# The last quarter of two down projections, from eight block products to seven

## The chip, the cores and the metric

The kernel runs on one core of a Trainium2 chip. The engines are TensorE (PE in the profile; its weight loads are PEld), VectorE (DVE), ScalarE (ACT), GpSimd (POOL) and SyncE (SP, which only issues DMAs here). The metric is the device time of one execution in microseconds; before the change the median of three runs is 987.07 us (986.94 to 987.56).

## The reference

The program computes two layers of a decoder on 512 tokens of width 1024, in float32. Layer 0 mixes with latent attention, layer 1 with sliding-window attention. After each mixer stands a feed-forward part, the one that the change touches:

```python
for l in range(DEPTH):                       # DEPTH = 2
    y = mixer_l(x)                           # latent attention, then banded attention
    x = layernorm(alpha * x + y, ...)
    x = layernorm(alpha * x + mlp(x, w_up[l], w_down[l]), ...)

def mlp(x, w_up, w_down):                    # 1024 -> 4096 -> 1024
    h = relu(x @ w_up)
    return (h * h) @ w_down
```

## The kernel before, in words

**Precision by split parts.** Nearly all matmuls are in a reduced fp32 format. To keep precision, each operand is split into a high and a low part: ScalarE copies the source into the format (the high part, line 77), and VectorE or GpSimd subtracts it from the source (the low part, line 81). A product is then three matmuls: high by high, high by low, low by high (`three`, line 109; all matmuls are issued on line 105). The order of the PE instructions is that of the program text: `pe` (line 86) keeps it. The instructions of the other engines are laid in order by a scheduler unless they are pinned the same way; SyncE's loads go through `pe` too.

**The feed-forward part, in blocks.** The hidden width of 4096 is cut into four blocks `q` of 1024. For each, the up product (named U) and the down product (named D) multiply a 2 by 2 arrangement of quarters by another one: tokens in two halves of 256, the inner width in two halves of 512, the outer in two halves of 512. A scheme of Strassen's kind does this in seven quarter products instead of eight: U'1 to U'7 and D1 to D7, each on sums and differences of quarters. Sums of activation quarters (`Factors.sum`, line 697) are made on VectorE; sums of weight quarters are made by DMAs that add as they land (`accum_op=ALU.add`, line 204, issued by GpSimd), one quarter onto the last in the same buffer (`queue_seven`, line 168). A quarter product of D is 2 token tiles by 4 inner tiles by 3 matmuls of 128x512; one of U is 24 pairs of 256-wide matmuls, that is 48.

**The order.** `FIRST_STEPS`, `STEPS` and `LAST_STEPS` (lines 39 and 40) write out the order of the quarter products: D of one block is woven with U of the next (the prime marks the next block). Weights pass through a ring of four split tiles: `weights` (line 336) prepares up to four entries of one stream ahead of the one in use, and an entry is split as soon as an older one is used up.

**The last block.** Block 3's down product has no next block to be woven with, and was not cut in seven. `LAST_STEPS` ends with U'6, U'7, U'4 and D4; after D6 the running sum `u2` is spread over the token tiles (`take`, `add_plain`); then `TokMajor(...).finish` (lines 521 to 590, called on line 955) multiplies four token tiles by the whole 1024 x 1024 weight block: 4 tiles x 2 halves of 512 columns x 8 inner tiles x 3 matmuls. Eight weight chunks of 512 KB are loaded for it. The first 512 columns run with the inner tiles outside, the second with the token tiles outside, so that each token tile is finished in turn and its layer norm (`layer_norm`, line 484) runs under the next tile's products. In layer 0 the transposes of tokens 0 and 1 for the next layer (`turn_tokens`, line 500) stand between the tiles. In layer 1 the last tile's second half is cut in two pieces of 256 columns, and `last_norm` (line 469) ends the kernel: two plain fp32 matmuls (lines 472 and 477) centre half of the tile on PE while VectorE does the other half.

Token tiles live in `xs[0..3]` (1024 columns each: `lows` are the first 512, `highs` the last); `stats` collects what the layer norm needs. PSUM has eight banks: six under the tag `mm`, two under `tr`.

Of the kernel before, what the change touches and what calls it, by code (L numbers as in the profile page):

```python
# [8 lines left out]
F32 = mybir.dt.float32  # L9
# [30 lines left out]
FIRST_STEPS, LAST_STEPS = "U'1 U'2 U'5 U'3 U'6 U'7 U'4 D'1 D'2", "U'1 D5 U'2 D3 U'5 D6 D7 U'3 U'6 U'7 U'4 D4"  # L40
# [8 lines left out]
def build(tc, nc, io, out):  # L49
    with ExitStack() as top:  # L50
# [6 lines left out]
        dr = top.enter_context(tc.tile_pool(name="dr", bufs=1, space=DRAM))  # L57

# [27 lines left out]
        def pe(ins):  # L86
            tc.keep_in_program_order(ins)
# [15 lines left out]
        def group(dst, pairs, first=True, last=True, **kw):  # L103
            for i, (st, mv) in enumerate(pairs):
                pe(nc.tensor.matmul(  # L105
                    dst, st, mv, start=first and i == 0, stop=last and i == len(pairs) - 1, **kw
                ))
# [174 lines left out]
        holds = []  # L282

        def mlp_stream(l):
# [7 lines left out]
            def down(q):  # L292
                return lambda r, c, jp: io["down"][l, q * 8 + 4 * c + 2 * (1 - r) + jp].rearrange(
                    "p (a b) -> p a b", a=2
                )

            add = {("U", q): queue_seven("up", "U", up(q)) for q in range(NFF)}
            add |= {("D", q): queue_seven("down", "D", down(q)) for q in range(NFF - 1)}
# [6 lines left out]
            for c in range(8):  # L305
                queue("down", io["down"][l, (NFF - 1) * 8 + c])
# [153 lines left out]
        def last_tokens(gb):  # L460
# [5 lines left out]
            nc.gpsimd.tensor_mul(xg, xs[NT - 1][:, 0:512], gb[0][:, 0:512])  # L466
            return minus, diag, xg, bank()

        def last_norm(gb, minus, diag, xg, b):

            x = xs[NT - 1]
            pe(nc.tensor.matmul(b, ident, xg, start=True, stop=False))
# [4 lines left out]
            pe(nc.tensor.matmul(b, diag, gb[0][:, 0:512], start=False, stop=True))  # L477
            late = slice(512, D)
            nc.vector.scalar_tensor_tensor(x[:, late], x[:, late], mv[:, 0:1], gb[0][:, late], ALU.subtract, ALU.mult)
            for c, src in ((late, x[:, late]), (slice(0, 256), b[:, 0:256]), (slice(256, 512), b[:, 256:512])):  # L480
                pin(nc.vector.scalar_tensor_tensor(x[:, c], src, r, gb[1][:, c], ALU.mult, ALU.add))
                nc.sync.dma_start(out[(NT - 1) * P : NT * P, c], x[:, c])

        def layer_norm(t, gb, dst):
# [9 lines left out]
            pin(nc.vector.scalar_tensor_tensor(x, x, mv[:, 0:1], gb[0], ALU.subtract, ALU.mult))  # L494
            state["norm"] = nc.vector.scalar_tensor_tensor(x, x, r, gb[1], ALU.mult, ALU.add)
            pin(state["norm"])
            if dst is None:
                nc.sync.dma_start(out[t * P : (t + 1) * P, :], x)
# [22 lines left out]
        class TokMajor:  # L521
# [25 lines left out]
            def finish(self, gb=None, dst=None, early=None, gb_at=None):  # L547
# [9 lines left out]
                if gb is not None:  # L557
# [3 lines left out]
                    for t in range(NT):  # L561
                        end = dst is None and t == NT - 1
                        n = 2 if end else 1
                        if end:
                            parts = last_tokens(gb)
                        for i in range(n):
                            c = slice(i * 512 // n, (i + 1) * 512 // n)
                            b = bank(512 // n)
                            for kp in range(4):
                                self.group(b, t, kp, ws[kp], c)  # L570
                            pinned[0] = early
                            with tc.high_priority():
                                self.evac(t, slice(512 + c.start, 512 + c.stop), b)
                            pinned[0] = False
                        pinned[0] = early
                        with tc.high_priority():
                            if end:
                                last_norm(gb, *parts)
                            else:
                                layer_norm(t, gb, dst)  # L580
                        if early:
                            prepare(early[t])
                        pinned[0] = False
                        if dst is not None and t in (1, 2):
                            with tc.high_priority():
                                dst.turn(t - 1)
# [9 lines left out]
        def run_steps(units, ahead, scores, turn, mix, fill, per, lag, rest):  # L596
# [5 lines left out]
            for u in range(-ahead, n):  # L602
# [9 lines left out]
                turn(*units[u])  # L612
                if u >= lag and (u - lag) % per == per - 1:
# [162 lines left out]
        def mlp(src, gb, dst, mp):  # L776
# [17 lines left out]
            class Block:  # L794
# [18 lines left out]
                def up(self, n):  # L813
# [4 lines left out]
                    key = {3: 3}.get(n) or own_bank[n]  # L818
                    for j in range(4):

                        b = self.bank(("U", key), j // 2)
                        wh, wl = w[j // 2]
                        for k in range(4):
                            c = slice(j % 2 * 512 + k * P, j % 2 * 512 + (k + 1) * P)
                            group(
                                b[:, j % 2 * 256 : j % 2 * 256 + 256],
                                three(wh[:, c], wl[:, c], src.part(n, 0)[:, k, :], src.part(n, 1)[:, k, :]),
                                n not in (2, 4) and k == 0 and j % 2 == 0, k == 3, skip_group_check=True,
# [838 lines left out]
```

## Time and profile before

| | |
|---|---|
| median of 3 runs | 987.07 us (986.94 to 987.56) |
| the profiled execution | 986.77 us, of which its span is 985.0 us |
| granted PE clock over the span | 1.000 |
| busy: PE, PEld, DVE, ACT, POOL | 978.4, 880.5, 773.4, 544.7, 235.7 us |
| DMA | 149.54 MB, mean 152 GB/s |
| last block of layer 0 with U'6, U'7, U'4, D4 before it | from 436.8 us |
| the same of layer 1 | 911.4 to 978.1 us |

Times in the views are microseconds from the span's start. A matmul's busy time overlaps the next one's, so a row's duration is not what it costs in a row of matmuls; that is the distance between starts. In views by window each engine's busy time is followed by its number of instructions. In the waits, the engine named after the arrow ended the idle time.

### The profile page before, as it was taken

How to read it: one execution, taken by the hardware profiler on the slowest of the kernel's cores; microseconds unless marked ns; L12 is line 12 of the kernel's file. 1: busy time of each engine (PE TensorE's matmuls, PEld its weight loads, DVE VectorE, ACT ScalarE, POOL GpSimd, SP SyncE). 2: the span in 40 equal slices, each digit the busy share in tenths (PEclk: the TensorE clock that was granted, in tenths of full speed). 3: DMA queues.
4: the chain of work that ended last, by engine and by line, in shares of the span. 5: the costliest groups of instructions: out<-in, count | busy, mean ns of one | idle time of the engine just before them, and what ended most of it. 6: DMA issues, size and time to landing. Idle time of an engine off the chain costs nothing.

```text
span 985.0 us, 15665 instructions
## 1 busy us (share of the span) xinstructions
PE 978.4 (99%) x6028; PEld 880.5 (89%) x6028; DVE 773.4 (79%) x1282; ACT 544.7 (55%) x842; POOL 235.7 (24%) x204
## 2 busy tenths in 40 slices
PE   9999999999999999999999999999999999999998
PEld 9888888998999999998898988889998998999986
DVE  6589858999778769887587788898886985888756
ACT  5557644467537637646136787445763763764720
POOL 1231101121212211310002898422221122033000
PEclk9999999999999999999999999999999999999999
DMA  7421236398878968973232212528997796897332
GB/s 264 146 89 44 91 124 199 59 225 218 156 181 235 183 141 237 226 125 120 94 108 86 97 65 98 191 44 181 256 179 134 236 197 117 225 264 140 82 128 86
DMA packets 60678, 149.54 MB, mean 152 GB/s; under 512 B 5259, under 2 KB 10300, under 8 KB 60604
## 3 DMA queue, kind: packets, MB, share of 16 engines
q0 software_dynamic: 24320, 58.73, 33.7%
q1 hardware_dynamic: 36140, 89.56, 26.0%
q8 instruction: 47, 0.77, 0.3%
q10 hardware_dynamic: 144, 0.26, 0.1%
q14 instruction: 27, 0.22, 0.1%
HBM read 146.41 MB, written 4.22 MB: 153 GB/s over the span
## 4 chain that ended last, share of the span: by engine, by line
PE 97%; DVE 2%; POOL 1%; ACT 0%; issue 0%; DVEq 0%; POOLq 0%
PE mm L105 89%; PE tr L105 5%; PE tr L1243 1%; PE tr L742 1%; POOL wl L81 1%; PE tr L1467 0%; PE tr L507 0%; DVE o L1503 0%; DVE mm L1431 0%; DVE pt L81 0%; PE tr L1007 0%; ACT wh L77 0%; DVE mm L1427 0%; PE mm L1148 0%; ACT p L1442 0%
## 5 line engine op out<-in xcount | busy, mean ns | idle before, releaser
L105 PE MATMUL mm<-wh,fac 128*128 128x512 f32 (+1 forms) x944 | 292.7, 386 | 0.0
L77 ACT ACTIVATE wh<-wq 128x1024 fp32r<-128x1024 f32 x164 | 173.7, 1060 | 184.7 <-PE mm L105 137.8
L81 DVE TENSOR_TENSOR wl<-wq,wh 128x1024 fp32r<-128x1024 f32 x164 | 199.2, 1220 | 67.5 <-ACT wh L77 66.6
L105 PE MATMUL mm<-xth,wh 128*128 128x256 f32 (+1 forms) x928 | 243.4, 290 | 0.0
L105 PE MATMUL mm<-xth,wl 128*128 128x256 f32 (+1 forms) x800 | 233.3, 292 | 0.0
L105 PEld LDWEIGHTS mm<-wh,fac 128*128 128x128 f32 x944 | 176.2, 188 | 35.5 <-DVE fac L81 0.6
L105 PE MATMUL mm<-xtl,wh 128*128 128x256 f32 (+1 forms) x672 | 197.1, 293 | 0.0
L105 PE MATMUL mm<-wl,fac 128*128 128x512 f32 (+1 forms) x472 | 182.3, 386 | 0.0
L105 PEld LDWEIGHTS mm<-xth,wh 128*128 128x128 f32 x928 | 168.6, 192 | 3.1
L105 PEld LDWEIGHTS mm<-xth,wl 128*128 128x128 f32 x800 | 153.2, 192 | 2.7
L105 PEld LDWEIGHTS mm<-xtl,wh 128*128 128x128 f32 x672 | 128.7, 191 | 3.0
L77 ACT ACTIVATE wh<-raw 128x1024 fp32r<-128x1024 f32 (+3 forms) x86 | 84.9, 989 | 79.3 <-PE mm L105 57.9
L204 POOL DMA_DIRECT2D wq<-in_up x64 | 77.6, 1238 | 200.3 <-DVE wl L81 193.0
L105 PEld LDWEIGHTS mm<-wl,fac 128*128 128x128 f32 x472 | 88.8, 188 | 16.6
L81 DVE TENSOR_TENSOR wl<-raw,wh 128x1024 fp32r<-128x1024 f32 (+2 forms) x64 | 74.3, 1169 | 30.6 <-ACT wh L77 29.6
L204 POOL DMA_DIRECT2D wq<-in_down x48 | 42.0, 874 | 189.1 <-DVE wl L81 183.2
L81 POOL TENSOR_TENSOR wl<-raw,wh 128x1024 fp32r<-128x1024 f32 (+2 forms) x22 | 47.1, 2143 | 90.8 <-ACT wh L77 65.2
L105 PE MATMUL mm<-wh,oh 128*128 128x512 f32 x128 | 50.7, 396 | 0.0
L105 PE MATMUL mm<-wl,oh 128*128 128x512 f32 x128 | 50.0, 391 | 0.2 <-POOL wl L81 0.2
L105 PE MATMUL mm<-wh,ol 128*128 128x512 f32 x128 | 50.2, 392 | 0.0
L443 POOL TENSOR_TENSOR rs<-mv,half 128x1 f32<-128x1 f32 x16 | 8.8, 552 | 168.1 <-DVE mv L488 163.4
L641 DVE TENSOR_TENSOR x<-mm,x 128x512 f32<-128x512 f32 (+1 forms) x49 | 32.9, 674 | 15.6 <-PE mm L105 15.5
(247 smaller groups left out, 1783.2 us busy)
## 6 DMA issues: line engine op xcount, KB each, us to landing
wq<-in_up POOLq DMA_DIRECT2D x64, 512.0 KB, 7.2
wq<-in_down POOLq DMA_DIRECT2D x48, 512.0 KB, 6.9
wq<-in_up SPq DMA_DIRECT2D x32, 512.0 KB, 6.8
raw<-in_down SPq DMA_DIRECT2D x28, 512.0 KB, 6.1
wq<-in_down SPq DMA_DIRECT2D x24, 512.0 KB, 5.9
raw<-in_up SPq DMA_DIRECT2D x16, 512.0 KB, 4.2
raw<-in_w_o SPq DMA_DIRECT2D x8, 512.0 KB, 3.3
raw<-in_w_sq SPq DMA_DIRECT2D x8, 512.0 KB, 3.2
```

The costliest lines, as they stand in the source:

```text
L77: high = nc.scalar.activation(dst_h, src, AF.Copy)
L81: low = (engine or nc.vector).tensor_sub(dst_l, src, f32(dst_h))
L105: pe(nc.tensor.matmul(dst, st, mv, start=first and i == 0, stop=last and i == len(pairs) - 1, **kw))
L204: state["added", key, a, more, jp] = nc.gpsimd.dma_start(half(a, jp), chunk(*more, jp), accum_op=ALU.add)
L443: state["rs"] = nc.gpsimd.tensor_tensor(r, v, half, ALU.pow)
L641: nc.vector.tensor_add(xs[t][:, c], b, xs[t][:, c])
L742: pe(nc.tensor.transpose(pt[:, a, :], xs[t][:, k * P : (k + 1) * P], ident))
L1243: pe(nc.tensor.transpose(pt[:, kb * P : (kb + 1) * P], p[:, kb * P : (kb + 1) * P], ident))
```

## The change

Both last blocks are now done in seven quarter products too, by a class `LastBlock`, in an order that `run` writes out for all engines.

- `LAST_STEPS` ends with D4. U'6, U'7 and U'4 of the last block are issued from the written plan, in halves (`up_half`), with their results' handling (`up_out`, `up_end`) as entries of their own.
- `run` is a list of (time, function) pairs, sorted by the time, which is only a key. While it is issued, all instructions of VectorE, ScalarE and GpSimd keep program order on their engine (class `Ordered`, flag `in_order`), not only PE's and SyncE's.
- The quarter products are 1, 2, 5, 3, 6, 7, each in two halves of one token tile (`times`, 12 matmuls), and the last one, on the quarter `a22`, in plain fp32: 4 matmuls a token tile on unsplit data (`low_left`); in layer 1 its second token tile is cut into two pieces of 256 columns.
- Sums that were made by adding results to `xs` afterwards are partly made in PSUM: ScalarE first copies `u2` or parts of `xs` into a bank (`into_bank`, `fill_end`), the product adds to it, and ScalarE copies results out (`copy_out`).
- The weights of products 1, 5 and 6 are one buffer that grows by accumulating DMAs (`grow`); those of 7 and of the plain product are sums which are prepared in DRAM: two plain copies and six accumulating DMAs, and two copies from DRAM to DRAM, a layer (`sum_quarters`), issued at written steps of the attention in layer 0 and of the feed-forward part in layer 1. `fetch` loads them.
- Of the twelve low parts of the weights, three (both of product 6, one of product 7) are made by GpSimd, as are four subtractions of token tiles' halves, three of them in the written plan's middle.
- Layer norms of the token tiles are cut in entries (`moments`, `centre`, `finish`). `last_norm` centres the second half of the last tile on PE instead of the first, and ScalarE and GpSimd scale and shift 256 columns of it, which ScalarE's queue stores.

The diff, cut to its core:

```diff
-FIRST_STEPS, LAST_STEPS = "U'1 U'2 ... D'2", "U'1 D5 U'2 D3 U'5 D6 D7 U'3 U'6 U'7 U'4 D4"
+FIRST_STEPS, LAST_STEPS = "U'1 U'2 ... D'2", "U'1 D5 U'2 D3 U'5 D6 D7 U'3 D4"
...
-                nc.vector.scalar_tensor_tensor(x[:, late], x[:, late], mv[:, 0:1], gb[0][:, late], ALU.subtract, ALU.mult)
-            for c, src in ((late, x[:, late]), (slice(0, 256), b[:, 0:256]), (slice(256, 512), b[:, 256:512])):
-                pin(nc.vector.scalar_tensor_tensor(x[:, c], src, r, gb[1][:, c], ALU.mult, ALU.add))
+            nc.vector.scalar_tensor_tensor(x[:, lows], x[:, lows], mv[:, 0:1], gb[0][:, lows], ALU.subtract, ALU.mult)
+            nc.scalar.activation(x[:, early], b[0], AF.Copy, scale=r)
+            nc.gpsimd.tensor_add(x[:, early], x[:, early], gb[1][:, early])
+            for c, src in ((lows, x[:, lows]), (late, b[1])):
+                nc.vector.scalar_tensor_tensor(x[:, c], src, r, gb[1][:, c], ALU.mult, ALU.add)
...
+                def product(self, b, f, t, w, first, cols=slice(0, 512)):
+                    tk = slice(t * P, (t + 1) * P)
+                    for m in range(4):
+                        if f is None:
+                            c = slice(m % 2 * 512 + cols.start, m % 2 * 512 + cols.stop)
+                            group(b, [(self.g["a22"][:, m, tk], w[m // 2][:, c])], False, m == 3, ...)
+                            continue
...
+            def sum_quarters(i, l, jp):
+            chunk = down(l, NFF - 1)
+            if i == 0:
+                pe(nc.sync.dma_start(sum_of(l, 7, jp), chunk(1, 1, jp)))
+            elif i == 1:
+                nc.gpsimd.dma_start(sum_of(l, 7, jp), chunk(0, 1, jp), accum_op=ALU.add)
+            elif i == 2:
+                pe(nc.sync.dma_start(sum_of(l, 4, jp), sum_of(l, 7, jp)))
+            else:
+                nc.gpsimd.dma_start(sum_of(l, 4, jp), chunk((0, 1)[i - 3], 0, jp), accum_op=ALU.add)
...
+            extra = sums_at(1, ((2, 2), (8, 14), (20, 20), (26, 32), (37, 43))) if layer else {}
...
+            todo = sums_at(0, ((0, 0), (3, 7), (12, 12), (13, 17), (21, 25)))
...
+                    at(8.7, self.factor_high, 3)
+                    at(9.18, self.factor_high, 6)
+                    at(10.28, self.grow, 6, 1, 1)
+                    at(10.85, self.into_bank, 5, 1, xs[1][:, highs])
+                    at(10.9, self.times, 5, 0, 5)
+                    at(13.27, self.copy_out, 1, 0, u2[0])
+                    at(13.28, self.high, 6, 0)
+                    at(13.28, self.high, 6, 1)
+                    at(13.6, self.times, 5, 1, 5)
+                    at(14.45, self.copy_out, 1, 1, u2[1])
+                    at(15.73, lambda: add_plain(2, highs, self.bank(("D", 5), 0)))
+                    at(15.73, self.fetch, 7)
+                    at(15.73, self.tops, 1)
+                    at(16.14, lambda: add_plain(3, highs, self.bank(("D", 5), 1)))
+                    at(16.3, self.times, 3, 0, 5)
+                    at(16.32, self.tops, 0)
...
+                    at(18.06, self.low, 6, 1, pool)
+                    at(19.0, self.times, 3, 1, 5)
+                    at(21.47, self.low, 6, 0, pool)
+                    at(21.8, self.times, 6, 0, 1)
+                    at(23.8, self.low, 7, 1, pool)
+                    at(27.2, self.times, 7, 0, 1)
+                    at(32.2, self.low_left, 0)
+                    at(34.6, self.times, 7, 1, 1)
+                    at(41.22, self.finish, 2)
+                    if end:
+                        at(38.0, self.low_left, 1, 0, 2)
+                        at(39.0, self.low_left, 1, 1, 2)
+                        at(39.44, self.left_out, 1, 0, 2)
+                        at(41.14, self.left_out, 1, 1, 2)
+                        at(42.58, lambda: parts.extend(last_tokens(self.gb)))
+                        at(44.0, lambda: last_norm(self.gb, *parts))
...
-            b = blocks[NFF - 1]
-            b.factor(2)
-            b.factor(1)
-            b.factor(4)
-            b.factor(0, True)
...
-            TokMajor(Hidden(), add_last, "down").finish(gb, dst, dst and (0, 0, 0, 1), 1)
-
+            in_order[0] = True
+            last.run(gb)
+            in_order[0] = False
```

More of the change, by code (lines that the diff above doesn't have):

```diff
@@ L46, with build @@
 C_ALL = 1024
-def build(tc, nc, io, out):
+def build(tc, core, io, out):
     with ExitStack() as top:
@@ L86, in pe @@
         def pe(ins):
-            tc.keep_in_program_order(ins)
+            if not (in_order[0] and ins.ins.engine in (mybir.EngineType.DVE, mybir.EngineType.Activation, mybir.EngineType.Pool)):
+                tc.keep_in_program_order(ins)
         pinned = [False]
@@ L290, in up @@
                 ].rearrange("c p x -> p c x")
[L292 to L295, printed above, removed]
             add = {("U", q): queue_seven("up", "U", up(q)) for q in range(NFF)}
[L298 removed]
+            add |= {("D", q): queue_seven("down", "D", down(l, q)) for q in range(NFF - 1)}
             preloads.append(add["U", 0].preload)
@@ L304, in mlp_stream @@
                     add[which, q](n)
-            for c in range(8):
-                queue("down", io["down"][l, (NFF - 1) * 8 + c])
+            for n in (6, 7, 4):
+                add["U", NFF - 1](n)
+            ends.append(len(stream))
         mlp_stream(0)
@@ L561, in finish @@
                     for t in range(NT):
[L562 to L575, printed above, removed]
-                        with tc.high_priority():
[L577 to L582, printed above, removed]
+                        b = bank()
+                        for kp in range(4):
+                            self.group(b, t, kp, ws[kp])
+                        pinned[0] = True
+                        with tc.high_priority():
+                            self.evac(t, slice(512, D), b)
+                        with tc.high_priority():
+                            layer_norm(t, gb, dst)
+                        prepare(early[t])
                         pinned[0] = False
-                        if dst is not None and t in (1, 2):
+                        if t in (1, 2):
                             with tc.high_priority():
@@ L612, in run_steps @@
                 turn(*units[u])
+                with behind([state["ex"]] if u in todo else None):
+                    for f in todo.get(u, ()):
+                        f()
                 if u >= lag and (u - lag) % per == per - 1:
@@ L817, in up @@
                     w.append(weights("up"))
-                    key = {3: 3}.get(n) or own_bank[n]
                     for j in range(4):
[L821 to L828, printed above, removed]
-                            )
+                        self.up_part(n, j, w[j // 2])
                         if j % 2:
                             self.up_out(n, j // 2)
+                            if j == 3:
+                                self.up_end(n)
                         if (self.q, n) == (0, 1) and j in (0, 3):
@@ L913, in mlp @@
+            blocks = [(LastBlock if q == NFF - 1 else Block)(q) for q in range(NFF)]
+            last = blocks[NFF - 1]
             steps = list(steps_of())
```

390 lines of the change are left out of this document (315 added, 75 removed).

## The prediction

> **What bounds the kernel now.** I read the engine shares and the chain first, then the two last blocks.
>
> ```profile
> span 985.0 us, 15665 instructions
> PE 978.4 (99%) x6028; PEld 880.5 (89%) x6028; DVE 773.4 (79%) x1282; ACT 544.7 (55%) x842; POOL 235.7 (24%) x204
> ...
> PE 97%; DVE 2%; POOL 1%; ACT 0%; issue 0%; DVEq 0%; POOLq 0%
> ```
>
> ```profile
> 436.00:503.00 67.00, 67.00 (x375) 58.52 (x374) 45.39 (x61) 26.37 (x28) 1.96 (x4) 1.00 0.31 94
> 911.00:978.00 67.00, 67.00 (x389) 59.24 (x388) 44.71 (x58) 22.33 (x22) 2.94 (x4) 1.00 0.30 95
> ```
>
> ```profile
> 911.38 5.76 PE tr L105 x48
> 917.13 61.01 PE mm L105 x336
> ...
> 978.17 0.43 DVE x L641
> ...
> 978.62 0.44 DVE bn L631
> ...
> 980.26 1.22 DVE x L481 x2
> ```
>
> TensorE (PE) is on 97% of the chain. The two windows cover the last block of each layer (columns: width, busy time of PE, weight load, VectorE, ScalarE, GpSimd, granted clock, DMA share, GB/s): PE never stops there, at full clock, while VectorE has 22 us free of 67. In the third view PE runs without a gap from U'6 (911.38) to 978.14. So time goes only as PE work goes, unless the new order makes PE wait; and after the last product there is a tail on VectorE.
>
> **The change, part by part.** *The matmuls.* Matmuls overlap, so the price is the distance of starts, not the duration.
>
> ```profile
> 959.75 0.62 PE L105 MATMUL mm<-wh,fac 128*128 128x512 f32 x2
> ...
> 960.43 0.62 PE L105 MATMUL mm<-wh,fac 128*128 128x512 f32 x2
> ...
> 977.37 0.28 PE L105 MATMUL mm<-wl,fac 128*128 128x256 f32 x1
> ...
> 977.73 0.28 PE L105 MATMUL mm<-wl,fac 128*128 128x256 f32 x1
> ...
> 977.96 1.02 PE L472 MATMUL mm<-xg,ident 128*128 128x512 f32 x2
> ```
>
> ```profile
> L472 PE MATMUL mm<-xg,ident x2: 592/592/593, 978.0 to 978.4; 128*128 128x512 f32 x2
> ```
>
> Three 512-wide matmuls of split parts take 960.43 - 959.75 = 0.68 us, 0.227 each; three 256-wide ones 0.36, 0.12 each. The one plain fp32 matmul in the kernel is two records that last 0.592 each and 1.02 together, so the second starts 0.43 after the first: 0.86 for a plain 512-wide matmul in a row of them, against 0.68 for the three that it replaces. Before, a layer's last block is 192 matmuls, 43.5 us (43.7 in layer 1, where the last 24 matmuls of 512 are halves: 24 x 0.12 in place of 12 x 0.227). After, it is six quarter products of 24, 144 x 0.227 = 32.7, and one of 8 plain matmuls, 8 x 0.86 = 6.9: 39.6. PE loses **3.9 us in layer 0 and 4.1 in layer 1**. Were a plain matmul only as dear as one split triple (0.68), it would be 5.3 and 5.5; at the bare duration of both records (1.18) it would be 1.4 and 1.6. I take 0.86, the start distance of this very form. Transposes and U'6, U'7, U'4 stay as many; D4 only moves ahead of U'6.
>
> *VectorE, ScalarE, GpSimd.*
>
> ```profile
> 929.83 1.22 DVE L81 TENSOR_TENSOR wl<-raw,wh 128x1024 fp32r<-128x1024 f32 x1
> 930.96 1.22 DVE L81 TENSOR_TENSOR fac<-a,fac 128x1024 fp32r<-128x1024 f32 x1
> ...
> 932.10 0.69 DVE L641 TENSOR_TENSOR x<-mm,x 128x512 f32<-128x512 f32 x1
> ```
>
> ```profile
> L81 POOL TENSOR_TENSOR wl<-raw,wh 128x1024 fp32r<-128x1024 f32 x14 | 34.7, 2477 | 58.6 <-ACT wh L77 35.6 <-PE mm L105 20.0 <-PE tr L1007 3.0
> ...
> L466 POOL TENSOR_TENSOR xg<-x,gb 128x512 f32<-128x512 f32 x1 | 1.3, 1282 | 46.0 <-DVE x L641 46.0
> ```
>
> ```profile
> 881.55 0.58 ACT L848 ACTIVATE a<-mm 128x512 f32<-128x512 f32 x1
> 883.46 1.06 ACT L77 ACTIVATE wh<-wq 128x1024 fp32r<-128x1024 f32 x1 [1.34 <-issue]
> ```
>
> A 1024-wide subtraction holds VectorE 1.13 us (start to start), a 512-wide one 0.6; ScalarE 1.06 and 0.58; GpSimd 2.48 and 1.28. Per block VectorE loses 8 low parts of weights and gets 9; 4 low parts of factors become 6; 4 sums of quarters are new, as are about two 512-wide adds: (1 + 2 + 4) x 1.13 + 1.2 = 9.1 us more. 45.4 + 9.1 of a window that shrinks to 63 is 87% busy: it fits, but each engine must now keep one written order. I walked that order with these durations, T = 0 at the first quarter product's first matmul. PE reaches product 2 at 5.4, 5 at 10.9, 3 at 16.3, 6 at 21.8, 7 at 27.2; the plain product's first half at 29.9. The tightest places: `factor_high(6)` on ScalarE waits for the third factor buffer until product 2 ends (10.9), then `into_bank(5,1)`, `copy_out(1,0)`, two highs of 6 and `copy_out(1,1)` end at 15.7; behind it on VectorE `tops(1)` runs to 17.1 and `add_plain(3)` to 17.7, and product 3's second half, which overwrites that bank, starts at 19.0. Its first half needs `add_plain(2)`, ready at 15.1, at 16.3. So the least cover is 1.2 us, and what is late beyond it PE waits for, one for one, as do all products behind. GpSimd's low parts of 6 run 15.2 to 20.1 against 21.8, that of 7 is done at 26 against 28.6. I count the waits at nothing by these covers, and put **0.5 us a layer** for what the walk can't see; the bounds are 0 and the 4.0 of the second rival.
>
> *DMA.* Per layer six accumulating transfers and four plain copies of 512 KB now build two sums in DRAM, in layer 0 during attention, in layer 1 during the MLP.
>
> ```profile
> q0 software_dynamic: 24320, 58.73, 33.7%
> q1 hardware_dynamic: 36140, 89.56, 26.0%
> ...
> wq<-in_up POOLq DMA_DIRECT2D x64, 512.0 KB, 7.2
> wq<-in_down POOLq DMA_DIRECT2D x48, 512.0 KB, 6.9
> ```
>
> ```profile
> 0.00:122.00 122.00, 121.01 (x676) 107.21 (x677) 95.31 (x276) 73.81 (x168) 24.68 (x26) 1.00 0.38 127
> ...
> 625.00:917.00 292.00, 291.81 (x1891) 267.20 (x1890) 240.64 (x265) 165.68 (x179) 68.83 (x63) 1.00 0.80 181
> ```
>
> All software transfers are the 112 accumulating ones: 0.337 x 985 / 112 = 3.0 us of all 16 engines each; a plain 512 KB is 0.26 x 985 x 0.524 / 89.56 = 1.5. So a layer gets 6 x 3.0 + 4 x 1.5 = 24 us. Layer 0's attention has 62% of 122 us free, layer 1's MLP 20% of 292, 58 us. No row shows an accumulation into DRAM; the upper bound I take is double, 48. Both fit on the whole, so 0. The cover of one late transfer is long: the weight split of 883.46 above had waited 1.34 us for its data, and, by the ring of four, it is U'5's second half, which PE reaches at 911.38 - 5.76 (U'3) - 2 x 24 x 0.227 (D7, D6) - 2.88 = 891.9, 6.0 us after its low part is out (883.46 + 1.06 + 1.3). GpSimd's issues and SyncE's loads are queued ahead by buffers, not by PE.
>
> *The tail.* The last block of layer 1 ends with left halves of 256 columns. `finish(2)` now stands on VectorE between the last token tile's statistics and their aggregation; before, it lay under PE work:
>
> ```profile
> 975.68 1.27 DVE L495 SCALAR_TENSOR_TENSOR x<-x,rs,gb 128x1024 f32<-128x1024 f32 x1
> ...
> 981.00 0.88 DVE L481 SCALAR_TENSOR_TENSOR x<-mm,rs,gb 128x256 f32<-128x256 f32 x2
> 981.04 1.30 SPq L482 DMA_DIRECT2D out<-x  x3
> ```
>
> That adds 1.27. One of two 256-wide steps (0.44) leaves VectorE for ScalarE and GpSimd; their path (diagonal product, 0.4 on ScalarE, about 0.65 on GpSimd, half of L466's 1.28) ends some 0.3 behind VectorE's. Sum **+0.9**, bounds 0.8 and 1.3.
>
> **Sum.** -3.9 - 4.1 + 1.0 + 0.9 = -6.1. The profiled execution took 986.77 us for its span of 985.0; 986.77 - 6.1 = 980.7. It lies 0.3 under the median of the runs (987.07), so **981.0**.
>
> **The rivals.** *GpSimd's subtractions hold VectorE up* (chance 0.15).
>
> ```profile
> 628.89 2.38 POOL L81 TENSOR_TENSOR wl<-raw,wh 128x1024 fp32r<-128x1024 f32 x1
> ...
> 629.15 3.21 DVE L81 TENSOR_TENSOR w_fac<-wq,w_fac 128x1024 fp32r<-128x1024 f32 x1
> ```
>
> Here a VectorE subtraction beside a GpSimd one took 3.21 us for 1.22: 2.0 lost. Three low parts a layer, each meeting one such subtraction, cost VectorE 6.0; the covers behind them (1.2 at product 3, 1.7 at 6, 2.6 at 7) leave perhaps 2 on PE: 981.0 + 2 x (2 - 0.5) = **984**. For it: the row. Against it: most VectorE work between T = 15 and 20 reads a bank, and such steps beside GpSimd keep their length. The Trainium skill (GPSIMD Engine Reference, Key points) says that GpSimd shares its SBUF interfaces with VectorE and collides with VectorE instructions that read two SBUF inputs; the trace agrees with its 3.21 us, and by that rule moving low parts to GpSimd frees VectorE of nothing while both read SBUF, and the time would be this rival's.
>
> *The written order makes ScalarE wait for a transfer* (0.10). `grow(6)` adds into a buffer that the highs of 6 read. If it went out where it stands, T = 10.3 and 11.2, and landed as late as this one:
>
> ```profile
> 909.70 1.20 POOL L204 DMA_DIRECT2D wq<-in_up  x1 [0.53 <-DVE wl L81]
> ...
> 917.92 1.06 ACT L77 ACTIVATE wh<-wq 128x1024 fp32r<-128x1024 f32 x1 [2.69 <-DMA wq<-in_up]
> ```
>
> 8.2 us later, the second high would end at 20.4, `copy_out(1,1)` at 21.0, `tops(1)` at 22.4, `add_plain(3)` at 23.0 against 19.0: 4.0 us a layer, 981.0 + 2 x 3.5 = **988**, no gain. Against it: only two subtractions stand ahead of it on GpSimd, and its buffer is free at 5.4.
>
> *The DMA engines fill up in layer 1* (0.15, slower). The mechanism is a backlog in the stretches with nothing free:
>
> ```profile
> 700.00:740.00 40.00, 40.00 (x246) 36.03 (x245) 34.36 (x34) 26.27 (x28) 10.07 (x10) 1.00 0.93 202
> ...
> 860.00:900.00 40.00, 40.00 (x245) 36.04 (x244) 33.07 (x34) 23.42 (x25) 10.08 (x10) 1.00 0.98 232
> ```
>
> The sums' steps 8, 26 and 37 fall into three such stretches, one a block. It decides from a delay of 6.0 us on, the cover above. At double price, with the copies of the neighbouring steps, a backlog of 10 leaves 4.0 on PE three times, 12.0: **993**. For it: shares of 0.93 and 0.98. Against it: the steps are six apart (over 30 us), and the stretches between have a quarter free.
>
> **How the numbers follow.** My forecast has 0.60; its own range is 979.0 (no waits, and plain matmuls a little cheaper) to 984. The first rival is still faster, the second within or just over the line, the third slower. A measurement here tells 0.2%, 2.0 us, from no change: faster is under 985.1, slower over 989.0. Faster 0.60 + 0.15 and a little of the second, 0.76; same 0.09; slower 0.15. The range leaves out the third rival and little else: from 977.2, no waits and plain matmuls at 0.68 (981.0 - 1.0 - 2.8), to 988.5, past the second rival; plain matmuls at 1.18 (986) lie inside.
>
> **What would show it.** Each last block has 144 matmuls of split parts, and 8 plain ones in 16 records (12 in 24 in layer 1, where four are halved), and the chain is still over 96% PE. A wait of PE on `x`, `u` or a bank from VectorE near product 3 means that the 1.2 us cover was short; subtractions of 2 to 3.2 us on VectorE beside GpSimd show the first rival; ScalarE waiting on a `wq` transfer ahead of the highs of 6 the second; PE waits on weights between 700 and 900 the third. The tail should run some 7.7 us from the last down matmul to the end, 6.8 before. I am wrong if a plain matmul's starts lie well off 0.43 apart.

## The result: 981.4 us, and the profile after

The changed kernel takes 981.41 us (median of four runs, 981.1 to 981.87) against 987.27 us for the kernel before beside it (986.94 to 987.56): a ratio of 0.9941, 95% interval 0.9924 to 0.9958. The forecast was 981.0. Run a second time on another occasion (called c_again below) it took 981.66 us (981.45 to 982.27), ratio 0.9942. The profiled execution took 981.28 us, 5.49 less than the one before. The total is right, but three of its terms are not: TensorE gained a little more than forecast, the waits that were allowed for did not come, and the tail lost 2.7 us instead of 0.9.

The page of the changed kernel, engine shares and shares of the chain:

```profile
span 979.4 us, 15632 instructions
PE 970.2 (99%) x5952; PEld 870.2 (89%) x5952; DVE 785.9 (80%) x1287; ACT 570.1 (58%) x884; POOL 278.9 (28%) x239
...
PE 94%; DVE 3%; DMA 1%; issue 1%; POOL 1%; ACT 0%; SPq 0%; POOLq 0%; DVEq 0%
```

The two last blocks as windows (width, then busy time of PE, weight load, VectorE, ScalarE, GpSimd, then granted clock, DMA share, GB/s), and two shorter ones from the end of layer 1's block:

```profile
436.00:501.00 65.00, 65.00 (x358) 54.68 (x356) 58.70 (x71) 41.90 (x51) 20.89 (x16) 1.00 0.61 177
907.00:970.00 63.00, 63.00 (x343) 54.04 (x343) 54.71 (x68) 36.34 (x44) 22.26 (x18) 1.00 0.59 161
...
937.00:952.00 15.00, 15.00 (x68) 12.43 (x67) 14.74 (x17) 9.41 (x13) 4.82 (x3) 1.00 0.48 123
...
962.00:969.70 7.70, 7.70 (x32) 5.85 (x32) 7.39 (x12) 0.60 (x1) 2.94 (x3) 1.00 0.25 100
```

PE is busy all through, as before. VectorE is busy 58.7 of 65 us in layer 0 and 54.7 of 63 in layer 1, where the prediction had worked out 54.5 of 63, and its free time is not spread: in layer 1 there are 0.3 us in the 15 us around product 3, and 0.3 us in the last 7.7. The chain of waits says the same (start, length, engine):

```profile
913.06 5.75 PE tr L126 x48
918.82 36.04 PE mm L126 x204
954.95 0.70 DVE x L69
...
966.23 1.92 DVE x L69 x2
968.23 1.27 POOL xg L69
969.50 2.73 issue
...
974.05 0.76 POOLq L1971
```

Before, the chain stayed on PE to the last product at 978. Now it leaves PE at 954.95, runs over VectorE, and ends on GpSimd's own closing instruction.

Matmuls matched one to one between the two traces show where the time went. The offset of the start of the same matmul, after minus before, is +0.66 us at the end of layer 0's attention; it falls from +0.66 to -3.68 across layer 0's last block (-4.34); it is -3.78 where layer 1's last block begins; it ends at -8.22 on the first matmul of `last_norm`, the first of the ident matmuls below (977.96 before, 969.74 after; -4.44 across the block). From that matmul to the end of the span the tail is 6.99 us before and 9.69 after: +2.70.

The tail of the changed kernel, by time (start, length, engine, operation; idle time before it and what ended that):

```profile
969.74 1.03 PE L496 MATMUL mm<-xg,ident 128*128 128x256 f32 x4
...
970.40 0.43 DVE L69 BATCH_NORM_STATS2 bn<-x 128x6 f32<-128x256 f32 x1
970.74 1.27 DVE L69 SCALAR_TENSOR_TENSOR x<-x,rs,gb 128x1024 f32<-128x1024 f32 x1
971.93 0.26 DVE L69 BATCH_NORM_AGGREGATE mv<-bn 128x2 f32<-128x24 f32 x1
...
974.08 0.72 POOL L69 TENSOR_TENSOR x<-x,gb 128x256 f32<-128x256 f32 x1 [1.25 <-ACT x L69]
974.84 0.35 ACTq L69 DMA_DIRECT2D out<-x  x1
```

And the closing instructions of GpSimd and SyncE, of the kernel after, and those of GpSimd in the kernel before (duration in ns, smallest, median and largest, first and last start):

```profile
L1971 POOLq DRAIN  x3: 40/93/4611, 974.0 to 979.2; - x3
L1971 SPq DRAIN  x3: 7/7/130, 977.2 to 978.9; - x3
```

```profile
L1663 POOLq DRAIN  x3: 40/102/3256, 979.4 to 984.7; - x3
```

The +2.70 has three pieces. Up to the aggregation it is +1.07: that is `finish(2)` (970.74). From the aggregation to the issue of the last store it is +0.1, where the prediction had taken 0.4 off. And +1.5 comes after the last store is issued: GpSimd's first closing drain begins at 974.05, lasts 4.61 us and ends at 978.66, while the last store has landed at 976.80. Before, the drain ended at 982.65, under the stores, the last of which landed at 984.00. Counted from the end of GpSimd's last instruction (979.98 before, 974.80 after) the drain takes 2.67 us before and 3.86 after; no term of the prediction held it. Not all of the 1.5 is the drain's: SyncE is through its own waits and its drain at 977.70, so GpSimd's drain holds the end up by 0.96 us. The other 0.6 lies in SyncE's closing waits, which run on for 0.9 us after the last landing, where they took 0.2 before.

### The profile page after: what moved, and what is told of

The parts are those of the page before. It is cut to its first block, busy times and chain, and to the rows that moved or that the text cites. A ratio compares the mean times of both kernels' runs of the same rounds, so it can differ in the third digit from the quotient of the medians.

```text
span 979.4 us, 15632 instructions
## 1 busy us (share of the span) xinstructions
PE 970.2 (99%) x5952; PEld 870.2 (89%) x5952; DVE 785.9 (80%) x1287; ACT 570.1 (58%) x884; POOL 278.9 (28%) x239
## 4 chain that ended last, share of the span: by engine, by line
PE 94%; DVE 3%; DMA 1%; issue 1%; POOL 1%; ACT 0%; SPq 0%; POOLq 0%; DVEq 0%
PE mm L126 86%; PE tr L126 5%; DMA sums<-in_down 1%; PE tr L1550 1%; DVE x L69 1%; PE tr L765 1%; PE tr L1775 0%; PE tr L539 0%; DVE o L1811 0%; DVE mm L1739 0%; POOL wl L101 0%; DVE bn L69 0%; DVE pt L101 0%; PE tr L1314 0%; DVE mm L1735 0%
## 5 line engine op out<-in xcount | busy, mean ns | idle before, releaser
L97 ACT ACTIVATE wh<-wq 128x1024 fp32r<-128x1024 f32 x158 | 167.3, 1060 | 183.3 <-PE mm L126 139.9
L101 DVE TENSOR_TENSOR wl<-wq,wh 128x1024 fp32r<-128x1024 f32 x158 | 192.1, 1221 | 79.2 <-ACT wh L97 78.7
L126 PE MATMUL mm<-wh,fac 128*128 128x512 f32 x736 | 232.2, 390 | 0.0
L126 PEld LDWEIGHTS mm<-wh,fac 128*128 128x128 f32 x736 | 138.3, 188 | 28.1
L126 PE MATMUL mm<-wl,fac 128*128 128x512 f32 x368 | 143.5, 390 | 0.0
L97 ACT ACTIVATE wh<-raw 128x1024 fp32r<-128x1024 f32 (+3 forms) x68 | 65.7, 970 | 38.0 <-PE mm L126 28.6
L126 PEld LDWEIGHTS mm<-wl,fac 128*128 128x128 f32 x368 | 69.2, 188 | 13.3
L101 DVE TENSOR_TENSOR wl<-raw,wh 128x1024 fp32r<-128x1024 f32 (+3 forms) x46 | 52.4, 1149 | 8.3 <-ACT wh L97 8.0
L126 PE MATMUL mm<-wx,fac 128*128 128x512 f32 x192 | 45.1, 392 | 0.0
L126 PEld LDWEIGHTS mm<-wx,fac 128*128 128x128 f32 x192 | 35.8, 188 | 7.7 <-DVE x L69 0.2
```

The costliest lines, as they stand in the source:

```text
L97: high = nc.scalar.activation(dst_h, src, AF.Copy)
L101: low = (engine or nc.vector).tensor_sub(dst_l, src, f32(dst_h))
L126: state["mm"] = nc.tensor.matmul(dst, st, mv, start=first and i == 0, stop=last and i == len(pairs) - 1, **kw)
```

## The experiments

Theory after the result: PE sets the time up to the last products, at the price of start distances; the covers on VectorE are as thin as walked; the tail is VectorE's work plus GpSimd's drain. Rivals: the drain is a sign only; the covers are wider; VectorE's room (55 of 63 us) would have carried more; the sums in DRAM cost something after all. Times are set against 981.41 and 981.66 of the changed kernel. Kernels that differ only in their end were up to 1.6 us apart ahead of it, so shifts of that size are read from the traces, by matched matmuls, and not from the medians alone.

**finish(2) ahead of the last half product.**

```diff
-                    at(41.22, self.finish, 2)
+                    at(39.0 if end else 41.22, self.finish, 2)
```

> finish(2) of layer 1 moved from behind the last token tile's statistics to before the last half product, under TensorE's work. Theory (the tail grew by two terms: finish(2) on VectorE's path, +1.1, and GpSimd's closing drain, +1.5, which hangs on GpSimd's last instruction): the tail falls from 9.7 to 8.6 us and the time by 1.1, to 980.3; the drain still ends last. Rival (GpSimd's drain alone sets the end, from something other than its last instruction, the stores in flight for instance): the tail stays at 9.7 and the time at 981.4. Second rival: VectorE has no 1.3 us to spare before the last half product, TensorE waits, and the time is 981.4 or more.

983.0 us (982.26 to 983.91), ratio 0.9957 [0.9943, 0.9970]. The tail is 10.16 us, 0.47 longer.

```profile
969.45 0.75 DVE L69 BATCH_NORM_STATS2 bn<-x 128x6 f32<-128x256 f32 x2
969.49 1.27 POOL L69 TENSOR_TENSOR xg<-x,gb 128x512 f32<-128x512 f32 x1 [0.28 <-DVE x L69]
970.12 1.73 DVE L69 SCALAR_TENSOR_TENSOR x<-x,rs,gb 128x1024 f32<-128x1024 f32 x1
971.02 1.03 PE L496 MATMUL mm<-xg,ident 128*128 128x256 f32 x4
971.77 0.41 DVE L69 TENSOR_TENSOR x<-mm,u 128x256 f32<-128x256 f32 x1
```

The theory falls and the second rival holds in part: PE did not wait, but there was no idle time on VectorE to put `finish(2)` into. Everything behind it, the additions of the last half product's results among it, came later, and beside a GpSimd multiplication it took 1.73 us for 1.27: the aggregation begins 2.64 us after the first ident matmul, 2.19 in the changed kernel. In this stretch VectorE, not PE, sets the time.

**The end without ScalarE's and GpSimd's share.**

```diff
-            nc.scalar.activation(x[:, early], b[0], AF.Copy, scale=r)
-            nc.gpsimd.tensor_add(x[:, early], x[:, early], gb[1][:, early])
-            for c, src in ((lows, x[:, lows]), (late, b[1])):
+            for c, src in ((lows, x[:, lows]), (early, b[0]), (late, b[1])):
...
-            nc.scalar.dma_start(out[(NT - 1) * P : NT * P, early], x[:, early])
```

> In last_norm the 256 columns of the end that went over ScalarE and GpSimd go over VectorE as the other 256 do, and SyncE issues all of the stores; nothing of the tail is left on GpSimd. Theory: GpSimd's closing drain then runs long before the end and the last store ends the kernel, as before the change; one more 256-wide step of 0.44 us on VectorE is paid back: the tail falls from 9.7 to some 8.2 us, the time by 1.1 to 1.6, to about 980.0. Rival (the drain is a sign and not the cause, and the stores themselves end later after the change): the tail stays at 9.7 or grows by 0.4, time 981.4 to 981.9.

981.86 us (980.64 to 982.24), ratio 0.9942 [0.9930, 0.9955]; the tail is 8.74 us, 0.95 shorter.

```profile
L1968 POOLq DRAIN  x3: 40/93/4454, 973.8 to 979.8; - x3
```

GpSimd's last instruction now ends at 974.43 and its drain, 3.86 us later again, at 978.29; the last store, issued at 976.34, lands at 978.40 and SyncE's closing waits end at 978.8. The last store lands 7.06 us after the first ident matmul in both kernels. So the drain is hidden, the tail shrinks although VectorE does 0.4 us more, and the drain was a cause and no sign. It gives 0.95 where 1.1 to 1.6 was expected, since SyncE's closing waits come right behind: from the issue of the last store to the end it is still 0.7 us longer than in the kernel before. The median shows none of it: the profiled run lost 1.6 us ahead of the tail, most of it in one place that is read below, under the run without sums.

**Both edits.**

> The edits of the two kernels above together. Theory (two separate terms): the tail falls to 7.1 us, about the 7.0 of the kernel before the change, and the time by 2.6, to 978.8. Rival (both are the same microseconds): the time is that of the better of the two, about 980.

981.33 us (980.75 to 982.78), ratio 0.9943 [0.9930, 0.9955]; the tail is 9.19 us. The two terms do not add, because the first is none: -0.95 from the end and +0.45 from `finish(2)` put where VectorE is full.

**finish(2) behind everything.**

```diff
-                    at(41.22, self.finish, 2)
+                    at(45.0 if end else 41.22, self.finish, 2)
```

> The changed kernel as it is, run again beside the three below, so that differences of 1 us are read on one chip. Expected on every theory: 981.4 within 0.6, and a tail of 9.7 us from the first ident matmul to the end.

> finish(2) of layer 1 moved behind last_norm, so that VectorE does it, and SyncE stores it, while GpSimd's closing drain runs. Theory (VectorE has no idle time ahead of the last token tile, so finish(2) is hidden only behind it; GpSimd's last instruction comes 1.19 earlier and the drain of 3.86 us with it): the tail falls from 9.7 to 8.5, the time by 1.2, to 980.2. Rival (the store of finish(2)'s 512 KB, issued some 2 us later than now, lands after the drain and ends the kernel): the tail falls by less than 0.5, time 981 or more.

982.13 us (981.58 to 982.49), ratio 0.9944 [0.9932, 0.9957], against 981.66 and 0.9942 for the kernel unchanged beside it, whose tail is 9.83 us. The tail here is 9.40.

```profile
974.55 0.72 POOL L69 TENSOR_TENSOR x<-x,gb 128x256 f32<-128x256 f32 x1 [1.25 <-ACT x L69]
974.78 1.58 DVE L69 SCALAR_TENSOR_TENSOR x<-x,rs,gb 128x1024 f32<-128x1024 f32 x1
975.31 0.35 ACTq L69 DMA_DIRECT2D out<-x  x1
976.38 0.33 SPq L1033 DMA_DIRECT2D out<-x  x1
```

The rival holds: the store of 512 KB goes out at 976.38 and lands at 979.01, in step with the drain (979.13), and the end gains 0.3 to 0.4. `finish(2)` costs its time wherever it stands. None of these four versions is faster than the changed kernel by more than its runs spread.

**VectorE held up ahead of product 3.** Four 512-wide statistics that nobody reads go in front of `add_plain(2)`, in both layers:

```diff
+                def hold_up(self, n):
+                    for _ in range(n):
+                        junk = sp.tile([P, 6], F32, tag="junk", bufs=4, name=nm("junk"))
+                        nc.vector.bn_stats(junk, self.gb[0][:, 0:512])
...
+                    at(15.72, self.hold_up, 4)
                     at(15.73, lambda: add_plain(2, highs, self.bank(("D", 5), 0)))
```

> Four added 512-wide statistics on VectorE, whose results nobody reads, ahead of add_plain(2) in both layers: VectorE, which has no idle time there, comes 4 x 0.66 = 2.6 us later to the bank that product 3 starts from. Theory (the least cover in the written order is 0.95 us at product 3's first half, as the trace of the changed kernel has it, and what is later TensorE waits for one for one): a wait of 1.7 us on VectorE in each layer ahead of product 3, +3.4 in all, 984.8. Rival (the cover is wider than that, the order has slack that the trace doesn't show): no wait and 981.4. Second rival (the delay is carried on through VectorE's order to products 6 and 7 and the end): +5 or more.

991.15 us (990.35 to 993.01), ratio 1.0041 [1.0027, 1.0055]. The jump ahead of product 3 is only 1.2 us in each layer; most of the rest, over 6 us, is a steady drift along the feed-forward parts, with no wait in it: the same 456 matmuls of one block take 73.55 us where they took 72.75 before the edit, and a 512-wide matmul starts 0.231 to 0.232 behind the last in place of 0.227. To separate the two, the same statistics were written into a tile that exists already (`kr`, of the attention), four of them and two:

```diff
-                        junk = sp.tile([P, 6], F32, tag="junk", bufs=4, name=nm("junk"))
-                        nc.vector.bn_stats(junk, self.gb[0][:, 0:512])
+                        kr = sp.tile([P, 2, 64], F32, tag="kr", bufs=2, name=nm("kr"))
+                        nc.vector.bn_stats(kr[:, 0, 0:6], self.gb[0][:, 0:512])
```

> Again four 512-wide statistics on VectorE ahead of add_plain(2) in both layers, 2.44 us as measured, now written into a tile that exists already, so that no tile's address moves. Theory A (the addresses moved by the 96 bytes a partition of the earlier kernel's own tile slowed its 512-wide matmuls, from 0.227 to 0.231 between starts): the starts are 0.227 apart again, TensorE waits 2.44 - 0.85 = 1.6 us ahead of product 3 in each layer (add_plain(2) is done 0.85 us ahead of its reader in the changed kernel's layer 0), and the time is 981.4 + 3.2 = 984.6. Theory B (the added work itself slows the matmuls): starts of 0.231 again and 990 or more.

> The same with two statistics, 1.22 us. Theory (a cover of 0.85 us, one for one beyond it): a wait of 0.4 us in each layer, 982.2. Rival (the cover is wider, or waits this short vanish): no wait, 981.4.

With four, 985.58 us (984.92 to 987.06), ratio 0.9981 [0.9972, 0.9991]; with two, 983.98 us (983.4 to 984.35), ratio 0.9963 [0.9950, 0.9977]. One block in the chains of the first run and of the second, both with four statistics:

```profile
213.30 73.55 PE mm L126 x456
```

```profile
213.27 72.75 PE mm L126 x456
```

And product 3's start, layer 0, in the second run:

```profile
474.95 2.46 DVE L69 BATCH_NORM_STATS2 kr<-gb 128x6 f32<-128x512 f32 x4
477.33 0.67 DVE L69 TENSOR_TENSOR x<-mm,x 128x512 f32<-128x512 f32 x1
...
478.05 0.50 PE L126 MATMUL mm<-wh,fac 128*128 128x512 f32 x1 [1.41 <-DVE x L69]
```

The jumps in the offset at this matmul are 1.58 us (layer 0) and 1.57 (layer 1) for a delay of 2.44, and 0.39 in each layer for one of 1.22: in all four cases the delay less 0.83 to 0.87. The walked cover is real, 0.85 us where the prediction said 1.2, and beyond it PE loses one for one. (The first run's jumps are 0.4 smaller for the same delay; PE itself had fallen 0.45 us behind within the block by then, which fits.) The pace is back with the tile gone, so theory B falls: the added work is not the cause, and the added tile is. That it acts through the addresses of other tiles, as theory A has it, is the likely way and was not shown. With four the whole time is 3.9 us longer, of which the jumps are 3.2. With two it is 2.3 us longer, of which about 0.8 are the jumps; the rest lies ahead of the last blocks, most of it in attention, and in the tail, and is not explained by the edit.

**Half of the plain product.** Every second inner tile is left out in both layers, so the output lacks half of that product.

```diff
+                        if f is None and m % 2:
+                            continue
...
```

> Every second inner tile of the plain product is left out in both layers: 4 in place of 8 plain matmuls of 512 columns (in layer 1 two of the four as halves). Theory (a plain matmul costs its start distance, 0.86 us, and TensorE sets the time there): 4 x 0.86 = 3.4 a layer, 6.9 in all, 974.5. Rival prices: 0.68 (as a triple of split parts) gives 976.0, 1.18 (the duration of both records) 972.0. Another rival (VectorE's work behind the last products sets the end of the block): less than 5 us gained and TensorE waiting on VectorE at the end of the block.

983.25 us (981.38 to 983.96), ratio 0.9952 [0.9939, 0.9965]: nothing gained. Yet the price is right to the digit. Over the two halves of the plain product the offset falls by 3.44 us in layer 0 and 3.41 in layer 1, 4 x 0.86. Then it is lost. The waits of PE (engine and what it waited for, us, times, longest):

```profile
PE mm L496 <- POOL xg L69: 3.0, 1, 3.0
PE mm L126 <- DVE xtl L69: 2.4, 1, 2.4
```

The last rival holds. Behind the plain product stand, in layer 0, layer 1's first matmuls, which need low parts (`xtl`) from VectorE, and in layer 1 `last_norm`, which needs `xg` behind VectorE's layer norms; both come hardly earlier than in the whole kernel: the low part 0.5 us and the first matmul of `last_norm` 0.2, with the run's own offset ahead of each block taken off. And a wait of 2.4 us cost more than 2.4:

```profile
498.00:500.00 2.00, 0.00 (x0) 0.00 (x0) 1.97 (x5) 0.73 (x1) 0.00 (x0) 1.00 0.00 0
500.00:502.00 2.00, 1.72 (x9) 1.72 (x10) 1.93 (x6) 0.00 (x0) 0.00 (x0) 0.68 0.00 0
502.00:504.00 2.00, 2.00 (x12) 2.00 (x11) 1.96 (x5) 0.00 (x0) 0.16 (x1) 0.50 0.65 164
504.00:506.00 2.00, 2.00 (x18) 2.00 (x18) 2.00 (x2) 0.00 (x0) 0.39 (x1) 0.97 0.28 98
```

After the stop the granted clock is 0.50 for some 3.4 us, in which 256-wide matmuls start 0.21 apart in place of 0.12: another 1.6 us. The gain of 3.4 is turned into a loss of 0.7 in layer 0.

**The plain product from split parts.** Two weight highs and a factor high more on ScalarE, two weight lows and a factor low more on VectorE, three matmuls for each plain one:

```diff
...
+                    at(22.2, self.factor_high, 4)
+                    at(22.21, self.high, 4, 0)
+                    at(22.22, self.high, 4, 1)
+                    at(22.3, self.low, 4, 0, vector)
+                    at(22.31, self.factor_low, 4)
+                    at(22.32, self.low, 4, 1, vector)
...
-                    self.product(b, None, t, [x.rearrange("p a b -> p (a b)") for x in self.raw[4]], False, c)
+                    self.product(b, self.fac[4], t, self.w[4], False, c)
...
```

> The plain fp32 product is made of split parts like the other six: three matmuls of 0.227 us for each plain one of 0.86, and for it two weight highs and one factor high on ScalarE, two weight lows and one factor low on VectorE. Theory (TensorE alone sets the time of the block; VectorE at 55 of 63 us has room for 3.4 more): 8 x (0.86 - 0.68) = 1.4 less in layer 0 and 1.3 in layer 1, 978.7. Rival (the buffers of the parts or VectorE's order toward the end make TensorE wait): the gain is lost, 981.4 or more, and TensorE waits on weights or factors ahead of the last product.

991.72 us (990.37 to 993.75), ratio 1.0041 [1.0028, 1.0054]: ten slower.

```profile
PE mm L126 <- DVE x L69: 6.6, 2, 3.8
```

```profile
488.00:490.00 2.00, 0.00 (x0) 0.00 (x0) 2.00 (x3) 0.00 (x0) 0.00 (x0) 1.00 0.00 0
490.00:492.00 2.00, 0.97 (x2) 0.83 (x3) 1.90 (x5) 0.00 (x0) 0.07 (x1) 0.65 0.00 0
492.00:494.00 2.00, 2.00 (x6) 1.59 (x5) 1.97 (x3) 0.00 (x0) 0.50 (x1) 0.50 0.00 0
```

The plain matmul's extra 0.18 does come back (the offset falls by 0.6 to 0.7 over a product half), but ahead of product 7 PE stops for 3.8 us in layer 0 and 2.8 in layer 1, and runs at half clock after each stop, 1.4 to 1.5 us more. The places given to the added entries were poor: in layer 0 the layer norm's first addition, which product 7 waits for, comes 5.4 us later than in the changed kernel, and 2.1 of these are VectorE standing idle for ScalarE's high parts with the layer norm queued behind. The rest is VectorE's own added work. So the plain product is worth what it spares VectorE and ScalarE; that a better place for the split parts would lose nothing was not tried.

**GpSimd's three low parts on VectorE.**

```diff
-                    at(18.06, self.low, 6, 1, pool)
+                    at(16.51, self.low, 6, 1, vector)
...
-                    at(21.47, self.low, 6, 0, pool)
+                    at(16.5, self.low, 6, 0, vector)
...
-                    at(23.8, self.low, 7, 1, pool)
+                    at(22.2, self.low, 7, 1, vector)
```

> The three low parts that the written order gives to GpSimd go to VectorE, in both layers, each 1.13 us there. Theory (VectorE is busy 55 of 63 us and the three have more than 2 us of cover): 981.4, within 0.5. Rival (GpSimd's part is needed: VectorE comes late to products 6 and 7): slower by 1 to 4 us, with TensorE waiting on VectorE near product 6 or 7. Second rival (GpSimd's subtractions hold VectorE up by more than they take from it): faster by 0.5 or more.

983.93 us (983.03 to 986.45), ratio 0.9960 [0.9946, 0.9974], some 2 us slower. In the trace layer 0's block loses 0.7 us ahead of product 7 and 0.75 ahead of layer 1's first matmuls, layer 1's block nothing; the rest of that run's loss lies outside the blocks. The first rival holds in layer 0: even 3.4 us more on VectorE is too much there.

**No sums in DRAM.** The accumulating transfers and copies are left out, and products 7 and 4 read a single quarter in place of a sum of quarters, so these additions are missing from the output.

```diff
-                        of = [sum_of(layer, n, jp) for jp in range(2)]
+                        of = [self.chunk(*{7: (0, 1), 4: (0, 0)}[n], jp) for jp in range(2)]
...
-            extra = sums_at(1, ((2, 2), (8, 14), (20, 20), (26, 32), (37, 43))) if layer else {}
+            extra = {}
...
-            todo = sums_at(0, ((0, 0), (3, 7), (12, 12), (13, 17), (21, 25)))
+            todo = {}
```

> The sums of quarter weights in DRAM are left out: the 12 accumulating transfers and 8 copies of them, and the products that use a sum read a single quarter in its place (so the kernel leaves out these additions). Theory (the DMA engines have room for them): 981.4, less 0.2 at the most that layer 0's attention lost. Rival (they hold other transfers up, in layer 1's MLP at a share of 0.9 above all): 980.5 or less, with waits of TensorE or a later start of the last block gone.

980.61 us (979.89 to 980.66), ratio 0.9925 [0.9911, 0.9939]: 0.8 to 1.1 us less (1.7 by the ratios), where the theory allowed 0.2. Matched with the changed kernel, no matmul from 640 us to the last one is moved by more than 0.1. The difference is in the tail, 9.04 us:

```profile
L1971 POOLq DRAIN  x3: 40/102/3954, 974.0 to 978.4; - x3
```

GpSimd's drain ends 3.20 us after its last instruction in place of 3.86. So the sums cost nothing on PE in that run, and 0.66 at the very end, by way of the drain. But in five of the other kernels' traces PE loses between 0.2 and 1.0 us at one place of layer 1's feed-forward part, about 792. The chain of the run with the end on VectorE (above) names it:

```profile
765.77 10.56 DMA sums<-in_down
...
777.37 13.09 DMA wq<-in_down
790.54 1.07 ACT wh L97
791.63 1.24 DVE wl L101
792.91 43.25 PE mm L126 x257
```

A weight transfer that stands behind the accumulations, itself an accumulating one, lands 13.1 us after its issue, and PE waits for the low part made from it. Without the sums the same transfer is issued some 6 us earlier, as no sum stands before it on GpSimd, and lands in 6.6 us, at 776.7. The cover there is used up within a microsecond: with each run's own offset taken off, the transfer lands at 788.1 and 788.9 in the two traces of the changed kernel, which lose nothing, and at 789.1 to 789.9 in the five that lose.

## Why the prediction was right, and where it was not

**The matmuls: right, a little small.** -3.9 and -4.1 us were forecast, -4.34 and -4.44 measured. The price that carried the sum, a plain matmul at 0.86 us by the distance of its records, is what the chip does:

```profile
489.97 3.60 PE L126 MATMUL mm<-wr,a 128*128 128x512 f32 x8
493.40 0.27 PE L539 MATMUL tr<-ident,x 128*128 128x128 f32 x1
```

Four plain matmuls in eight records take 493.40 - 489.97 = 3.43, 0.86 each; the half product above takes off exactly as much. Of the 0.4 too little in layer 0, some 0.2 are four starts of 0.27 to 0.34 in the kernel before, where the prediction had counted 0.227, against one such start after; in layer 1 two such starts give 0.15. The rest stays open.

**The waits: the allowance was not needed.** 0.5 us a layer was put down for what the walk could not see; PE waits for nothing inside either block. The walk held within 0.4 us: `add_plain(2)` was forecast ready at T = 15.1 against a reader at 16.3, and the two controlled delays put that cover at 0.85 us. "What is late beyond it PE waits for, one for one" holds for the stops of 0.4 and 1.6 us there; behind the stops of 2.4 us and more in the other runs the half clock adds to the wait.

**"87% busy: it fits": true, and misleading.** VectorE's total was 1 to 2 us too small: the 45.4 is layer 0's, whose block has 56.7 us in the 63 from 436 on, not 54.5; layer 1's 44.7 + 9.1 = 53.8 came to 54.7. It fits, yet 3.4 us more of work, or 3.4 us less of PE, both fail, because the 6 to 8 us that are left lie where nothing can use them. The kernel has gone as far as PE alone can take it: half of the plain product can be left out without a gain.

**The tail: the step that failed.** "Sum +0.9, bounds 0.8 and 1.3" measured +2.70. Two things were wrong in it. The 0.4 for one 256-wide step that leaves VectorE was not saved, as ScalarE's and GpSimd's path ends 0.42 us behind VectorE's; by the prediction's own 0.3 only 0.14 of the 0.44 could be saved, and its sum should have been 1.1. And what follows the last store had no term: +1.5. GpSimd's closing drain, which in the kernel before ended 1.4 us ahead of the last landing, was moved to the end by giving GpSimd a last instruction that ends 2.0 us later than before, counted from the aggregation, and had grown from 2.67 to 3.86 us; the run with the end on VectorE puts its cost at 0.95. The remaining 0.6 to 0.7 are SyncE's closing waits, which stayed in that run; why they are longer was not tried. The row of the drain stood in the trace before, hidden, and was not read. One of the prediction's signs failed with the tail: the chain was to be over 96% PE and is 94%. The Trainium skill (VectorE: DVE Perf Modes, The DRAIN you can't avoid) tells of closing drains of about 12 ns on every engine; here that is about true of the other engines' last ones (7 to 19 ns), and GpSimd's first ends 2.67 to 3.86 us after its last instruction.

**DMA and the start.** "0" for the DMA engines holds for the profiled run, and the third rival's mechanism was there all the same: weights behind the sums land late ahead of 792, with a loss of 0 to 1.0 us in place of its 12. That transfer lands 11.3 to 13.1 us later than without the sums, half of it by a later issue. The rival was to decide from a delay of 6.0 on; the cover at this place took about 12, and the delay cost time at one place and not at three. Of the transfers the prediction missed eight accumulations:

```profile
wq<-in_down POOLq DMA_DIRECT2D x56, 512.0 KB, 7.6
...
sums<-in_down POOLq DMA_DIRECT2D x12, 512.0 KB, 8.2
```

The +0.66 us up to the end of layer 0's attention were not forecast. The run without sums has them too, so the sums are not their cause, and runs of nearly the same program differ there by as much.

**The first rival** (GpSimd's subtractions hold VectorE up) was real in kind and small:

```profile
945.32 4.77 POOL L69 TENSOR_TENSOR wx<-wq,wx 128x1024 fp32r<-128x1024 f32 x2 [8.27 <-ACT wx L69]
...
949.40 1.77 DVE L69 TENSOR_TENSOR wx<-wq,wx 128x1024 fp32r<-128x1024 f32 x1
```

0.55 us lost on one subtraction of 1.22 in each layer, not 2.0 on three; moving the low parts back to VectorE made the kernel slower, not faster. The second rival's wait of ScalarE on a transfer ahead of the highs of 6 did not occur.

Altogether +0.66 - 4.34 - 0.10 - 4.44 + 2.70 = -5.5 was measured where -3.9 - 4.1 + 1.0 + 0.9 = -6.1 was forecast. That the total came this close is partly luck: 1.8 us too little in the tail and the 0.66 at the start stood against 0.8 too little of gain and 1.0 of waits that did not come.

## What to carry to other kernels

Price a chain of matmuls by the distance of starts of the same form, and walk the written order of the engine that feeds it; both held to a few tenths here. Before counting a gain beyond the forecast, ask which engine is next: leaving out 3.4 us a layer of TensorE work gained nothing, since VectorE was full at the end of the block. And read the closing instructions of every engine in the trace before giving an engine work in the last microseconds: a drain that is hidden before a change can end the kernel after it.

## What the runs showed of the hardware, unexpected

- GpSimd's closing drain ends a fixed time after its last instruction: 3.86 us in every run of the changed kernel and its variants with all transfers, 3.20 with the twelve accumulations of the sums left out, 2.67 in the kernel before. GpSimd issues 132, 120 and 112 DMAs in these three; that the drain grows with their number fits, and no run isolated it.
- A stop of TensorE of 2.4 us (and of 2.8 and 3.8) was followed by a granted clock of 0.50 for about 3.4 us; after one of 1.4 it stayed at 1.00, and after the 2.0 ahead of the last four matmuls it was 1.00 in one run of the changed kernel and 0.50 in the other. The Trainium skill (TensorE: Matmul & The Clock Gate, HAM oscillation — how this bites in real kernels) warns of gaps over some 3.4 us; here stops of 2.4 and 2.8 us already cost 1.4 to 1.6 us each.
- With one tile of 96 bytes a partition more in SBUF (four buffers of 24) the 512-wide matmuls of split weights start 0.231 to 0.232 apart in place of 0.227, 0.8 us in 456 matmuls and over 6 us in the kernel, and writing into an old tile instead undid it. Whether it acts by the addresses of other tiles, and of which, was not tried.
